# Attention queries: the second operand's marks and maxima transposed two heads at a time, its high parts copied by VectorE, and side b prepared further ahead

## The chip, the cores and the metric

One Trainium2 chip, one core. The metric is device time in microseconds of the whole kernel, one launch. Times of a kernel are the median of several executions; a profile is taken of one further execution, whose own time stands beside them.

## The reference

A decoder layer on 1024 tokens of 1024 channels. After an adaptive layer norm, one projection gives the queries, keys, values and gates of two attention branches. The NSA branch (8 heads, 2 key heads, here "side a") adds three attentions: over compressed keys, over the 8 blocks of 64 keys that the compressed scores pick, and over a window of 512. The SWA branch ("side b") has a window of 128 and one sink logit per head. Both are gated, merged, projected and normalised. What the change touches is the softmax of the last two kinds:

```python
s = einsum('bqghd,bkgd->bghqk', qb, kb) * dh ** -0.5
s = where(mask, s, NEG_INF)
p = softmax(concatenate([s, sink]))[..., :-1]   # side b; side a without sink
o = einsum('bghqk,bkgd->bqghd', p, vb)
```

All inputs and outputs are float32. The kernel computes in float32 accuracy by splitting operands in a high and a low part.

## The kernel before

The stages in time: projections of keys and compression (to 141 us), the attention of side a (to about 616 us), of side b (to about 726 us), then the branches' outputs, the merge and the last norm. Attention is the class `Att` (from L719). A unit is one side, one key head (group) and one tile of 128 queries, with 4 heads; there are 16 units in each side. Key tiles hold 128 keys.

Three things happen to each unit, each written as a generator that yields its estimated TensorE time:

- `C` (L744): the unit's queries `q` are split into a high part (ScalarE, L752) and a low part (GpSimd, L753) in `qat`; 4 transposes (L759) put both, heads side by side, into one PSUM bank; ScalarE copies it to `qa` (L761). ScalarE also copies `q` into columns 0 to 63 of `qbt` (L755). In side a, compressed attention and the selection follow, which write marks of the blocks that aren't selected to columns 64 to 79 of `qbt`.
- `M` (L829): scores with the queries as the stationary side (matmuls by L108, the helper of all matmuls), whose row maxima VectorE takes from the bank (L878) to `mx` and reduces into columns 80 and 81 of `qbt` (L882). 4 transposes of `qbt` (L890) fill one bank and ScalarE copies it to `qb` (L892). So `qb` holds q's high part, marks and maxima as rows.
- per key tile, `score` (L896): two matmuls, `qa` and `qb` against two operands of the keys, add up to the scores less the row maximum; on the diagonal and at the window's edge VectorE adds a mask (L907); ScalarE takes Exp (L909, L911) and the high part `ph` (L914), GpSimd the low part `pl` (L917). `weigh` (L920): 12 matmuls of `pl`, `ph` with V. `combine` (L940): VectorE divides by the sum.

`run` (L960) writes the order: at each step the score one step ahead, then parts of M of the next unit and of C of the unit behind it, then the weighing, and after each piece as much "fill" as a ratio asks: projections of queries, side b's keys (`kv_b`), and gate projections (`gm_block`, L1246, whose result `gmo` VectorE copies out and SP's queue writes). A framework then orders instructions by their dependences and puts semaphores. Banks 2 to 4 turn over among C, M and their transposes, 0 and 1 among the scores, 5 holds the weighed sums, 6 and 7 the fill. `qb` has 2 buffers, `qa` 3, `qbt` 2. The factor 0.125 of the scores is in the tables (`qcos`, `qsin`, L1173) with which queries are rotated. The core of `run`:

```python
            if ui + 1 < len(units):
                part(self.M, units[ui + 1], k, n)
            if ui + 2 < len(units):
                part(self.C, units[ui + 2], k, n)
```

Of the kernel before, what the change touches and what calls it, by code (L numbers as in the profile page):

```python
# [7 lines left out]
F32 = mybir.dt.float32  # L8
F32R = mybir.dt.float32r
# [4 lines left out]
OP = mybir.AluOpType  # L14
# [701 lines left out]
class Att:  # L716


    def __init__(self, L, q, work):  # L719

        self.L, self.q, self.w = L, q, work
        self.ms, self.st, self.av = Banks(L, MS), Banks(L, ST), Banks(L, (5,))
        nc = L.nc
        self.nc = nc
        self.U = {}
        self.qbt = []
        for i in range(2):
# [3 lines left out]
        self.p0 = work.tile([128, 128], F32, name="p0")[:, :68]  # L731
        nc.gpsimd.memset(self.p0, 0.0)
        self.n, self.last = 0, []
        self.off = [True, True]

    def rows_off(self, i):

        if not self.off[i]:
            self.nc.gpsimd.tensor_copy(self.qbt[i][:, :, 64:80],
                                       self.L.mk[:, 128:129, None].to_broadcast([128, 4, 16]))  # L740
            self.off[i] = True


    def C(self, u):  # L744
# [5 lines left out]
        self.n += 1  # L750
        qbt = st["qbt"] = self.qbt[self.n % 2]
# [8 lines left out]
        qa = st["qa"] = w.tile([128, 512], F32R, name="qa", tag="qa", bufs=3)  # L760
        nc.scalar.copy(qa, tr.bitcast(F32).rearrange("p h t -> p (h t)"))  # L761
        yield 0.25
        if side == "b":
            self.rows_off(self.n % 2)
# [5 lines left out]
        t = w.tile([128, 4, 64], F32, name="cs", tag="cs")  # L770
        nc.vector.tensor_tensor(t, sc[:, :, 1, :], L.vis[:, qt, None, :].to_broadcast([128, 4, 64]), op=OP.add)
        nc.vector.tensor_tensor(t, t, sc[:, :, 0, :], op=OP.add)
        sm = w.tile([128, 4, 8], F32, name="csm", tag="csm", bufs=2)[:, :, :4]
# [8 lines left out]
        pc = w.tile([128, 4, 64], F32, name="cp", tag="cp")  # L782
        nc.vector.scalar_tensor_tensor(pc.rearrange("p h c -> p (h c)"), e.rearrange("p h c -> p (h c)"), TINY,
# [5 lines left out]
        if qt >= 4:  # L789
            nc.vector.tensor_reduce(self.p0[:, 1:64], pc[:, :, 0:63].rearrange("p h c -> p c h"), axis=AX.X, op=OP.add)  # L790
            im = w.tile([128, 4, 16], F32, name="imp", tag="imp")
# [3 lines left out]
            m8 = w.tile([128, 40], F32, name="m8", tag="m8")[:, :8]  # L795
            nc.vector.max(m8, im[:, 1])
            nc.vector.match_replace(im[:, 2], m8, im[:, 1], -3e38)
            sel = st["sel"] = w.tile([128, 16], F32, name="sel", tag="sel", bufs=3)
            nc.vector.tensor_scalar(sel, im[:, 2], -2e38, NEG, op0=OP.is_gt, op1=OP.mult)
            nc.gpsimd.tensor_copy(qbt[:, :, 64:80], sel[:, None, :].to_broadcast([128, 4, 16]))  # L800
# [7 lines left out]
        pT = w.tile([128, 2, 128], F32, name="pT", tag="pT")  # L808
        nc.scalar.copy(pT, tp)
# [19 lines left out]
    def M(self, u):  # L829
        L, nc, w = self.L, self.nc, self.w  # L830
        side, g, qt = u
        st = self.U[u]
        qa, qbt = st["qa"], st["qbt"]
        brs = self.branches(u)
# [5 lines left out]
        for bi, (br, kts) in enumerate(brs):  # L840
# [10 lines left out]
            for a, b, hs in groups:  # L851
# [29 lines left out]
                yield 0.22 * (b - a) * len(hs) / 512  # L881
        nc.vector.tensor_reduce(qbt[:, :, 80:82], mx, axis=AX.X, op=OP.max, negate=True)  # L882
        if side == "b":
            es = st["es"] = w.tile([128, 2, 4], F32, name="esink", tag="esink", bufs=3)
            nc.gpsimd.tensor_tensor(es[:, 0], L.sink[:, g * 4:g * 4 + 4], qbt.bitcast(F32)[:, :, 80 + g], op=OP.add)
            nc.scalar.activation(es[:, 1], es[:, 0], AF.Exp, bias=L.poff)
        yield 0
        tr = self.ms.tile([128, 4, 128], F32R)
        for h in range(4):
            self.last.append(nc.tensor.transpose(tr[:, h, :], qbt[:, h, :], L.idr).ins)  # L890
        qb = st["qb"] = w.tile([128, 512], F32R, name="qb", tag="qb", bufs=2)
        nc.scalar.copy(qb, tr.bitcast(F32).rearrange("p h t -> p (h t)"))  # L892
        yield 0.25


    def score(self, u, br, kt):  # L896
# [9 lines left out]
        if kt == qt or edge:  # L906
            nc.vector.tensor_tensor(e.rearrange("p (h q) -> p h q", h=4), ps.rearrange("p (h q) -> p h q", h=4),  # L907
                                    L.mkt[:, int(edge), None, :].to_broadcast([128, 4, 128]), op=OP.add)
            nc.scalar.activation(e, e, AF.Exp, bias=L.poff)  # L909
        else:  # L910
            nc.scalar.activation(e, ps, AF.Exp, bias=L.poff)  # L911
        ph = w.tile([128, 512], F16, name="ph", tag="ph", bufs=PB)
# [47 lines left out]
    def run(self, units, fill, ratio, values):  # L960
# [80 lines left out]
        for gi, grp in enumerate(groups):  # L1041
# [24 lines left out]
            if k == n:  # L1066
                if ui + 1 < len(units):
                    finish(self.M, units[ui + 1])
                if ui + 2 < len(units):
                    finish(self.C, units[ui + 2])  # L1070
                self.U.pop(u)
                fill.done(u)
# [51 lines left out]
def run_layer(L):  # L1124
# [69 lines left out]
    def q_chunk(side, g, rows):  # L1194
# [322 lines left out]
```

## Time and profile before

| what | value |
|---|---|
| median of 3 runs | 943.93 us (943.79, 943.93, 946.45) |
| profiled execution | 945.29 us, of which the span of the core's instructions is 943.5 us |
| mean granted clock of TensorE in it | 0.994 of full speed |
| TensorE (PE) busy | 914.3 us |
| VectorE (DVE), ScalarE (ACT), GpSimd (POOL) busy | 550.2, 471.4, 575.6 us |

Busy times are of the one profiled execution; engines work side by side, so they don't add up to the span. PEld is TensorE's loading of stationary operands, which overlaps its matmuls. The granted clock (PEclk) is 1.00 at 2.4 GHz and 0.50 at 1.2 GHz.

### The profile page before, as it was taken

Reading aid. Unit: us, or ns where it says so; the run is one execution under the profiler, and the core shown is the slowest. Engines: PE = TensorE matmul, PEld = TensorE weight load, DVE = VectorE, ACT = ScalarE, POOL = GpSimd, SP = SyncE. Lnnn points to the kernel's source line nnn. Section 1 sums busy time; section 2 is a strip of 40 time slices with the busy share of each in tenths; the row PEclk is TensorE's granted clock in tenths of the full one; section 3 lists DMA queues with packets and bytes.
Section 4 is the critical chain, followed back from the end, with each engine's and each line's share of the span. In section 5 each row is a group of like instructions: output and inputs, shape, how many; then the busy total and the mean of one; then the engine's idle time right before and its main releaser. Section 6 shows DMA issues by size and latency. Waiting matters only on the chain.

```text
span 943.5 us, 18610 instructions
## 1 busy us (share of the span) xinstructions
PE 914.3 (97%) x6592; PEld 787.0 (83%) x6592; DVE 550.2 (58%) x1621; ACT 471.4 (50%) x984; POOL 575.6 (61%) x808
## 2 busy tenths in 40 slices
PE   7899998999999999999999999999899999999996
PEld 5689997788899888898899888789788888888885
DVE  7843356554776554465786643456552666454687
ACT  5846344344555566646555555756663664532100
POOL 7867565365768766767677766756753245535822
PEclk9999999999999999999999999999989999999999
DMA  9913232212202211202201212030222977655312
GB/s 329 293 29 115 81 91 57 79 51 79 68 7 53 62 57 57 63 13 70 76 7 35 74 58 75 22 101 13 69 62 75 371 249 221 192 188 193 130 69 110
DMA packets 93278, 95.40 MB, mean 101 GB/s; under 512 B 7616, under 2 KB 72192, under 8 KB 93184
## 3 DMA queue, kind: packets, MB, share of 16 engines
q1 hardware_dynamic: 93184, 94.21, 31.9%
q8 instruction: 52, 0.85, 0.4%
q14 instruction: 42, 0.34, 0.1%
HBM read 73.21 MB, written 20.97 MB: 100 GB/s over the span
## 4 chain that ended last, share of the span: by engine, by line
PE 69%; DMA 8%; DVE 8%; POOL 7%; ACT 3%; issue 3%; SPq 1%; DVEq 0%; POOLq 0%; ACTq 0%
PE bank L108 65%; DMA sg<-gm_raw 2%; POOL z L1421 2%; DMA raw<-in_w_ada_dram 2%; DMA raw<-in_w_out_dram 1%; DMA raw<-in_w_in_dram 1%; POOL rstd L1444 1%; DVE res L1450 1%; POOL pl L917 1%; PE bank L890 1%; DVE jk L878 1%; DMA x<-in_x_dram 1%; PE bank L759 1%; POOL whl L260 1%; PE bank L1327 1%
## 5 line engine op out<-in xcount | busy, mean ns | idle before, releaser
L108 PE MATMUL bank<-whl,uH 128*128 128x256 f32 (+3 forms) x1168 | 270.6, 322 | 4.6 <-ACT uH L449 4.3
L108 PE MATMUL bank<-uH,whl 128*128 128x512 f32 x768 | 247.5, 397 | 0.0
L917 POOL TENSOR_TENSOR pl<-e,ph 128x512 f16<-128x512 f32 x162 | 188.1, 1167 | 66.4 <-ACT ph L914 58.1
L108 PEld LDWEIGHTS bank<-whl,uH 128*128 128x128 f32 x1168 | 197.9, 189 | 22.2 <-ACT uH L449 5.3
L108 PE MATMUL bank<-whl,uL 128*128 128x256 f32 (+3 forms) x584 | 181.3, 319 | 0.0
L108 PEld LDWEIGHTS bank<-uH,whl 128*128 128x128 f32 x768 | 142.1, 189 | 26.8
L260 POOL TENSOR_TENSOR whl<-raw,whl 128x256 fp32r<-128x256 f32 x128 | 99.1, 779 | 86.6 <-ACT whl L259 78.6
L108 PE MATMUL bank<-uL,whl 128*128 128x512 f32 x384 | 151.3, 394 | 0.0
L108 PEld LDWEIGHTS bank<-whl,uL 128*128 128x128 f32 x584 | 110.1, 189 | 7.4
L914 ACT CAST ph<-e 128x512 f16<-128x512 f32 x162 | 98.4, 618 | 25.1 <-PE bank L108 23.1
L878 DVE CUSTOM_DVE_ANT_0 jk<-bank,mk 128x256 bf16<-128x256 f32 (+3 forms) x168 | 73.9, 440 | 30.0 <-PE bank L108 25.4
L911 ACT ACTIVATE e<-bank,poff 128x512 f32<-128x512 f32 x92 | 62.0, 687 | 54.0 <-PE bank L108 50.3
L108 PEld LDWEIGHTS bank<-uL,whl 128*128 128x128 f32 x384 | 72.6, 189 | 14.9
L259 ACT CAST whl<-raw 128x256 fp32r<-128x256 f32 x128 | 50.8, 404 | 66.0 <-PE bank L108 42.2
L108 PE MATMUL bank<-yH,whl 128*128 128x512 f32 x256 | 79.1, 393 | 0.0
L108 PEld LDWEIGHTS <-pl 128*128 128x128 f16 x648 | 59.4, 98 | 17.1 <-issue 11.2
L249 POOL TENSOR_TENSOR whl<-raw,whl 128x256 fp32r<-128x256 f32 (+3 forms) x60 | 53.3, 895 | 24.1 <-ACT whl L248 22.8
L907 DVE TENSOR_TENSOR e<-bank,mkt 128x512 f32<-128x512 f32 x70 | 47.5, 688 | 33.0 <-PE bank L108 27.9
L108 PEld LDWEIGHTS <-ph 128*128 128x128 f16 x1296 | 65.2, 97 | 0.8 <-issue 0.5
L909 ACT ACTIVATE e<-e,poff 128x512 f32<-128x512 f32 x70 | 49.8, 721 | 30.5 <-DVE e L907 30.2
L248 ACT CAST whl<-raw 128x256 fp32r<-128x256 f32 (+3 forms) x72 | 34.2, 480 | 60.9 <-DMA raw<-in_w_out_dram 36.8
L108 PEld LDWEIGHTS bank<-yH,whl 128*128 128x128 f32 x256 | 47.7, 188 | 10.1 <-issue 0.5
(292 smaller groups left out, 1730.0 us busy)
## 6 DMA issues: line engine op xcount, KB each, us to landing
raw<-in_w_in_dram SPq DMA_DIRECT2D x136, 128.0 KB, 2.2
gm_raw<-gmo SPq DMA_DIRECT2D x48, 256.0 KB, 2.0
wada<-in_w_ada_dram SPq DMA_DIRECT2D x16, 512.0 KB, 6.0
sg<-gm_raw SPq DMA_DIRECT2D x32, 256.0 KB, 3.2
x<-in_x_dram SPq DMA_DIRECT2D x8, 512.0 KB, 5.1
o_raw<-q SPq DMA_DIRECT2D x32, 128.0 KB, 1.9
o<-o_raw SPq DMA_DIRECT2D x8, 512.0 KB, 6.7
z<-gm_raw SPq DMA_DIRECT2D x16, 256.0 KB, 6.7
```

What stands on the lines that cost most here:

```text
L108: return self.nc.tensor.matmul(out, l, r, start=start, stop=stop, skip_group_check=True)
L248: self.cast = nc.scalar.copy(h, raw).ins
L249: low = eng.tensor_tensor(l, raw, h.bitcast(F32), op=OP.subtract).ins
L259: nc.scalar.copy(hl[:, 0], raw)
L260: eng.tensor_tensor(hl[:, 1], raw, hl.bitcast(F32)[:, 0], op=OP.subtract)
L878: nc.vector.tensor_tensor_reduce(o, src, m, 1.0, -3e38, OP.add, OP.max, mx[:, h, g if side == "b" else bi, slots[h]:slots[h] + 1])
L907: nc.vector.tensor_tensor(e.rearrange("p (h q) -> p h q", h=4), ps.rearrange("p (h q) -> p h q", h=4), L.mkt[:, int(edge), None, :].to_bro ...
L909: nc.scalar.activation(e, e, AF.Exp, bias=L.poff)
L911: nc.scalar.activation(e, ps, AF.Exp, bias=L.poff)
L914: nc.scalar.copy(ph, e)
L917: eng.tensor_tensor(pl, e, ph, op=OP.subtract)
L1421: nc.gpsimd.tensor_scalar(z[:, t, :], z[:, t, :], ALPHA, None, op0=OP.mult)
```

## The change

- `qbt` goes. Marks and maxima have a small tile `ex` of 32 columns per head (16 marks, 2 maxima, zeros), 2 of them in side a, 3 in side b. `qb` becomes a persistent buffer (3 in side a, 4 in side b) whose rows 64 to 127 are zeroed once by VectorE.
- The high parts, rows 0 to 63 of `qb`, are now copied by VectorE from C's transposed bank (64x512, L788 of the new kernel), the bank that ScalarE copies to `qa` (L787). ScalarE's cast of `q` (L755) goes.
- M's transposes take two heads at a time: 2 of 128x64 (L916) for 4 of 128x128; two VectorE copies of 32 rows and 2x128 columns (L920) put the result into `qb`, and ScalarE's copy (L892) goes. The yield of this piece is 0.14 for 0.25.
- The factor 0.125 moves from the rotation tables, which go with their three multiplications on ScalarE, into the `scale` of Exp; sinks are multiplied by 8 once on GpSimd.
- Some temporaries of side a lie in a pool of their own, closed at the first C of side b, where a second pool gives the additional `qb`, `ex` and `qa`.
- In side b a function `jobs` names what is written at which step: for unit ui the rest of M of ui+1, the score groups of M of ui+2, and C of ui+3. Before it was M of ui+1 and C of ui+2.

```diff
-        self.qbt = []
-        for i in range(2):
-            q = work.tile([128, 4, 128], F32R, name=f"qbt{i}")
-            nc.gpsimd.tensor_copy(q.rearrange("p h d -> p (h d)"), L.mk[:, 128:129].to_broadcast([128, 512]))
-            self.qbt.append(q)
+        self.ex = [work.tile([128, 4, 32], F32R, name=f"ex{i}") for i in range(2)]
+        self.qb = [work.tile([128, 512], F32R, name=f"qb{i}") for i in range(3)]
+        for x in self.ex:
+            nc.gpsimd.tensor_copy(x.rearrange("p h c -> p (h c)"), L.mk[:, 128:129].to_broadcast([128, 128]))
+        for x in self.qb:
+            nc.vector.tensor_copy(x[64:128], L.mk[64:128, 128:129].to_broadcast([64, 512]))
...
+        if side == "a":
+            ex, qb = self.ex[self.n % 2], self.qb[self.n % 3]
+        else:
+            if len(self.ex) == 2:
+                L.close(self.wx_cm)
+                self.wx, self.wx_cm = L.pool("sideb", 1, side="right")
+                self.qb.append(self.wx.tile([128, 512], F32R, name="qb3"))
+                self.ex.append(self.wx.tile([128, 4, 32], F32R, name="ex2"))
+                nc.gpsimd.tensor_copy(self.ex[2].rearrange("p h c -> p (h c)"), L.mk[:, 128:129].to_broadcast([128, 128]))
+                nc.vector.tensor_copy(self.qb[3][64:128], L.mk[64:128, 128:129].to_broadcast([64, 512]))
+                self.nb = 0
+            i = (1, 2, 0)[self.nb % 3]
+            if i < 2:
+                self.rows_off(i)
+            ex, qb = self.ex[i], self.qb[(2, 3, 0, 1)[self.nb % 4]]
+            st["n"] = self.nb
+            self.nb += 1
+        st["ex"], st["qb"] = ex, qb
         nc.scalar.copy(qat[:, :, 0, :], q)
...
-        (nc.gpsimd.tensor_copy if QL == 2 else nc.scalar.copy)(qbt[:, :, 0:64], q)
...
+        if side == "b" and st["n"] % 4 == 1:
+            qa = self.wx.tile([128, 512], F32R, name="qa3", tag="qa3")
+        else:
+            qa = w.tile([128, 512], F32R, name="qa", tag="qa", bufs=3)
+        st["qa"] = qa
         nc.scalar.copy(qa, tr.bitcast(F32).rearrange("p h t -> p (h t)"))
+        nc.vector.tensor_copy(qb[0:64], tr.bitcast(F32)[0:64].rearrange("p h t -> p (h t)"))
...
-        nc.scalar.activation(e, t, AF.Exp)
+        nc.scalar.activation(e, t, AF.Exp, scale=SCALE)
...
-        nc.vector.tensor_reduce(qbt[:, :, 80:82], mx, axis=AX.X, op=OP.max, negate=True)
+        nc.vector.tensor_reduce(ex[:, :, 16:18], mx, axis=AX.X, op=OP.max, negate=True)
...
-        tr = self.ms.tile([128, 4, 128], F32R)
-        for h in range(4):
-            self.last.append(nc.tensor.transpose(tr[:, h, :], qbt[:, h, :], L.idr).ins)
-        qb = st["qb"] = w.tile([128, 512], F32R, name="qb", tag="qb", bufs=2)
-        nc.scalar.copy(qb, tr.bitcast(F32).rearrange("p h t -> p (h t)"))
-        yield 0.25
+        tr = self.ms.tile([128, 2, 128], F32R)
+        for j in range(2):
+            self.last.append(nc.tensor.transpose(tr[0:64, j, :], ex[:, 2 * j:2 * j + 2, :].rearrange("p h c -> p (h c)"),
+                                                 L.idr).ins)
+        rows = qb[64:96].rearrange("p (j i t) -> p i j t", j=2, i=2)
+        for i in range(2):
+            nc.vector.tensor_copy(rows[:, i], tr.bitcast(F32)[i * 32:i * 32 + 32])
+        yield 0.14
...
+        def all_but(f, u):
+            s = get(f, u)
+            while s[1] < 3:
+                s[1] += 1
+                feed(next(s[0]))
...
+        def jobs(ui):
+            b = 2 * NT
+            if ui == b - 2:
+                return [(finish, self.C, b + 1, 0)]
+            if ui == b - 1:
+                return [(finish, self.M, b, -6), (finish, self.C, b + 2, -3), (all_but, self.M, b + 1, -1)]
+            if ui >= b:
+                e = EORD
+                return [(finish, self.M, ui + 1, e[0]), (all_but, self.M, ui + 2, e[1]), (finish, self.C, ui + 3, e[2])]
+            return []
 
...
-            if ui + 1 < len(units):
+            if ui < 2 * NT - 1:
                 part(self.M, units[ui + 1], k, n)
-            if ui + 2 < len(units):
                 part(self.C, units[ui + 2], k, n)
+            for f, g, x, w in jobs(ui):
+                if x < len(units) and k == (w if w > 0 else n + w):
+                    f(g, units[x])
...
+    nc.gpsimd.tensor_scalar(L.sink, L.sink, 1.0 / SCALE, None, op0=OP.mult)
...
-    L.qcos = qp.tile([128, 8, 32], F32, name="qcos")
-    qsin = qp.tile([128, 2, 8, 32], F32, name="qsin")
-    L.qsin = (qsin[:, 0], qsin[:, 1])
-    for o, x in ((L.qcos, L.cos), (L.qsin[0], L.nsin), (L.qsin[1], L.sin)):
-        nc.scalar.mul(o, x, 0.125)
```

TensorE's instructions in side b, in the kernel before (`K·qa` as `qa,Kw` with 512 columns is the first score matmul, `qb,Kw` the second; `Kw,qa` are M's scores; `whl`, `uH`, `uL` are fill):

```order
L108 MATMUL bank_10418<-Kw_934,qa 128x256 x2
L108 MATMUL bank_10386<-uL,whl 128x512
L759 MATMUL bank_10472<-idr,qat 128x128 x4
L108 MATMUL bank_10459<-qa,Kw_934 128x512
L108 MATMUL bank_10502<-qa,Kw_934 128x512
L108 MATMUL bank_10518<-Kw_934,qa 128x256 x2
L890 MATMUL bank_10452<-idr,qbt_1882 128x128 x4
L759 MATMUL bank_10583<-idr,qat 128x128 x4
L108 MATMUL bank_10459<-qb,Kw_934 128x512
L108 MATMUL bank_10502<-qb,Kw_934 128x512
L108 MATMUL bank_10525<-Kw_934,qa 128x256 x2
```

Here C's transposes into bank_10472 stand three rows ahead of M's scores into bank_10518, which read the copy of that bank. And after the change, again in side b (L781 are C's transposes, L916 M's, of `ex`):

```order
L110 MATMUL bank_10482<-qb_1881,Kw_930 128x512
L110 MATMUL bank_10421<-uH,whl 128x512 x2
L110 MATMUL bank_10421<-uL,whl 128x512
L110 MATMUL bank_10421<-uH,whl 128x512 x2
L110 MATMUL bank_10421<-uL,whl 128x512
L110 MATMUL bank_10421<-uH,whl 128x512 x2
L110 MATMUL bank_10421<-uL,whl 128x512
L110 MATMUL bank_10527<-qa,Kw_930 128x512
L781 MATMUL bank_10503<-idr,qat 128x128 x4
L110 MATMUL bank_10588<-qa,Kw_930 128x512
L110 MATMUL bank_10543<-Kw_930,qa_10369 128x256 x2
L916 MATMUL bank_10492<-idr,ex_1879 64x128 x2
```

M's scores into bank_10543 read a `qa` whose transposes stand 69 rows earlier, with two steps' weighing and 18 fill matmuls between; the C at L781 between them belongs to a later unit. VectorE's instructions at a place in side b, before (`jk,mx` are M's maxima):

```order
L878 ISA jk,mx<-bank_10411,mk 128x256
L878 ISA mx 128x1
L878 ISA jk,mx<-bank_10411,mk 128x256
L878 ISA mx 128x1
L907 TENSOR_TENSOR e<-bank_10318,mkt 128x512
L907 TENSOR_TENSOR e<-bank_10395,mkt 128x512
L878 ISA jk,mx<-bank_10418,mk 128x256
L878 ISA mx 128x1
L878 ISA jk,mx<-bank_10418,mk 128x256
L878 ISA mx 128x1
```

Maxima and the masked adds of scores (`e`) take turns. After the change:

```order
L904 ISA jk,mx<-bank_10441,mk 128x256
L904 ISA mx 128x1
L920 CAST qb_1881<-bank_10356 32x2x128 x2
L788 CAST qb_8285<-bank_10364 64x512
L904 ISA jk,mx<-bank_10441,mk 128x256
L904 ISA mx 128x1
L935 TENSOR_TENSOR e<-bank_10425,mkt 128x512
L904 ISA jk,mx<-bank_10448,mk 128x256
L904 ISA mx 128x1
L976 TENSOR_TENSOR cf<-bank_10378,esink 128x4
L935 TENSOR_TENSOR e<-bank_10482,mkt 128x512
```

The new copies into `qb` stand between the maxima of one bank, and ahead of the masked add that follows.

## Rows read from the trace of the kernel before

**Rows 1.** Page, part 1: busy us (share of the span) xinstructions.

```profile
span 943.5 us, 18610 instructions
...
PE 914.3 (97%) x6592; PEld 787.0 (83%) x6592; DVE 550.2 (58%) x1621; ACT 471.4 (50%) x984; POOL 575.6 (61%) x808
```

**Rows 2.** Page, part 4: the chain that ended last, by engine.

```profile
PE 69%; DMA 8%; DVE 8%; POOL 7%; ACT 3%; issue 3%; SPq 1%; DVEq 0%; POOLq 0%; ACTq 0%
```

**Rows 3.** Stretches: length, busy us PE PEld DVE ACT POOL, PEclk, DMA, GB/s.

```profile
199.00:616.00 417.00, 415.66 (x3625) 359.62 (x3624) 242.68 (x872) 238.70 (x474) 289.49 (x378) 1.00 0.18 53
616.00:726.00 110.00, 105.50 (x909) 92.22 (x908) 57.21 (x211) 61.95 (x131) 63.88 (x102) 0.97 0.19 54
```

**Rows 4.** The same view, finer, in side b.

```profile
679.00:683.30 4.30, 2.08 (x13) 1.28 (x11) 2.46 (x10) 2.93 (x7) 2.42 (x6) 1.00 0.51 122
683.30:690.15 6.85, 6.46 (x29) 5.43 (x30) 3.17 (x10) 5.17 (x12) 5.73 (x9) 0.50 0.01 2
690.15:726.00 35.85, 35.44 (x285) 29.44 (x285) 15.07 (x54) 16.99 (x35) 15.52 (x21) 1.00 0.20 60
```

**Rows 5.** TensorE's waits, 616 to 726 us: total us, times, longest us.

```profile
PE bank L108 <- ACT qa L761: 1.5, 1, 1.5
PE bank L890 <- DVE qbt L882: 1.4, 3, 0.7
PE bank L759 <- DVE mx L878: 1.0, 1, 1.0
```

**Rows 6.** Timeline of TensorE: start us, us, instruction [idle before <-releaser].

```profile
679.02 0.46 PE L759 MATMUL bank<-idr,qat 128*128 128x128 f32 x4
679.32 1.06 PE L108 MATMUL bank<-qa,Kw 128*128 128x512 f32 x2
681.92 0.50 PE L108 MATMUL bank<-Kw,qa 128*128 128x256 f32 x2 [1.55 <-ACT qa L761]
682.26 0.45 PE L890 MATMUL bank<-idr,qbt 128*128 128x128 f32 x4
683.69 0.72 PE L759 MATMUL bank<-idr,qat 128*128 128x128 f32 x4 [0.97 <-DVE mx L878]
```

**Rows 7.** Timeline of TensorE in side b, at M's transposes.

```profile
645.32 0.46 PE L890 MATMUL bank<-idr,qbt 128*128 128x128 f32 x4
645.62 0.20 PE L108 MATMUL bank<-Vs,pl 128*128 128x65 f16 x1
```

**Rows 8.** Instructions on qbt: ns min/median/max, first and last start.

```profile
L890 PEld LDWEIGHTS bank<-idr,qbt x128: 138/141/147, 184.5 to 713.9; 128*128 128x128 f32 x128
```

**Rows 9.** Groups by line and form, whole span: busy us, mean ns | idle before.

```profile
L892 ACT CAST qb<-bank 128x512 fp32r<-128x512 f32 x32 | 18.8, 586 | 22.4 <-PE bank L890 22.2
...
L761 ACT CAST qa<-bank 128x512 fp32r<-128x512 f32 x32 | 18.6, 581 | 7.0 <-PE bank L759 6.8
...
L755 ACT CAST qbt<-q 128x256 fp32r<-128x256 f32 x32 | 13.1, 409 | 0.1
...
L310 DVE CAST Kw<-bank 64x256 fp32r<-64x256 f32 x12 | 5.1, 427 | 5.8 <-ACT Kw L309 5.6
...
L907 DVE TENSOR_TENSOR e<-bank,mkt 128x512 f32<-128x512 f32 x70 | 47.5, 688 | 33.0 <-PE bank L108 27.9 <-POOL pl L917 2.7 <-POOL mx L839 1.8
...
L909 ACT ACTIVATE e<-e,poff 128x512 f32<-128x512 f32 x70 | 49.8, 721 | 30.5 <-DVE e L907 30.2
...
L914 ACT CAST ph<-e 128x512 f16<-128x512 f32 x162 | 98.4, 618 | 25.1 <-PE bank L108 23.1
...
L917 POOL TENSOR_TENSOR pl<-e,ph 128x512 f16<-128x512 f32 x162 | 188.1, 1167 | 66.4 <-ACT ph L914 58.1 <-DVE mx L878 1.7 <-POOL pl L917 1.4
```

**Rows 10.** TensorE's waits, 141.5 to 199 us.

```profile
PE bank L108 <- ACT qa L761: 0.7, 1, 0.7
PE bank L890 <- DVE qbt L882: 0.6, 1, 0.6
```

**Rows 11.** Who waited for ScalarE's casts of L309, from keys' banks: us, times.

```profile
  DVE Kw L310: 5.6, 6
```

**Rows 12.** Groups of VectorE, 616 to 726 us.

```profile
L907 DVE TENSOR_TENSOR e<-bank,mkt 128x512 f32<-128x512 f32 x26 | 17.3, 687 | 9.1 <-PE bank L108 7.0 <-POOL mx L839 1.8 <-POOL pl L917 0.2
```

More of the change, by code (lines that the diff above doesn't have):

```diff
@@ L28 @@
 POFF = math.log(16.0)
+SCALE = 0.125
+EORD = (1,0,1)
 XB = 8
@@ L725, in __init__ @@
         self.U = {}
-        self.qbt = []
-        for i in range(2):
-            q = work.tile([128, 4, 128], F32R, name=f"qbt{i}")
-            nc.gpsimd.tensor_copy(q.rearrange("p h d -> p (h d)"), L.mk[:, 128:129].to_broadcast([128, 512]))
-            self.qbt.append(q)
+        self.ex = [work.tile([128, 4, 32], F32R, name=f"ex{i}") for i in range(2)]
[4 more added lines that the diff above has]
+            nc.vector.tensor_copy(x[64:128], L.mk[64:128, 128:129].to_broadcast([64, 512]))
         self.p0 = work.tile([128, 128], F32, name="p0")[:, :68]
+        self.wx, self.wx_cm = L.pool("sidea", 1, side="right")
         nc.gpsimd.memset(self.p0, 0.0)
@@ L738, in rows_off @@
         if not self.off[i]:
-            self.nc.gpsimd.tensor_copy(self.qbt[i][:, :, 64:80],
+            self.nc.gpsimd.tensor_copy(self.ex[i][:, :, 0:16],
                                        self.L.mk[:, 128:129, None].to_broadcast([128, 4, 16]))
@@ L750, in C @@
         self.n += 1
-        qbt = st["qbt"] = self.qbt[self.n % 2]
+        if side == "a":
[16 more added lines that the diff above has]
+        st["ex"], st["qb"] = ex, qb
         nc.scalar.copy(qat[:, :, 0, :], q)
@@ L769, in C @@
                              L.kcd[:, g].rearrange("p i c -> p (i c)"), True, True).ins)
-        t = w.tile([128, 4, 64], F32, name="cs", tag="cs")
+        t = self.wx.tile([128, 4, 64], F32, name="cs", tag="cs")
         nc.vector.tensor_tensor(t, sc[:, :, 1, :], L.vis[:, qt, None, :].to_broadcast([128, 4, 64]), op=OP.add)
         nc.vector.tensor_tensor(t, t, sc[:, :, 0, :], op=OP.add)
-        sm = w.tile([128, 4, 8], F32, name="csm", tag="csm", bufs=2)[:, :, :4]
+        sm = self.wx.tile([128, 4, 8], F32, name="csm", tag="csm", bufs=2)[:, :, :4]
         nc.vector.tensor_reduce(sm[:, 0], t, axis=AX.X, op=OP.max)
@@ L781, in C @@
         nc.gpsimd.tensor_tensor(e, e, sm[:, 2, :, None].to_broadcast([128, 4, 64]), op=OP.mult)
-        pc = w.tile([128, 4, 64], F32, name="cp", tag="cp")
+        pc = self.wx.tile([128, 4, 64], F32, name="cp", tag="cp")
         nc.vector.scalar_tensor_tensor(pc.rearrange("p h c -> p (h c)"), e.rearrange("p h c -> p (h c)"), TINY,
@@ L790, in C @@
             nc.vector.tensor_reduce(self.p0[:, 1:64], pc[:, :, 0:63].rearrange("p h c -> p c h"), axis=AX.X, op=OP.add)
-            im = w.tile([128, 4, 16], F32, name="imp", tag="imp")
+            im = self.wx.tile([128, 4, 16], F32, name="imp", tag="imp")
             nc.vector.tensor_reduce(im[:, 0], self.p0[:, 0:64].rearrange("p (j i) -> p j i", i=4), axis=AX.X, op=OP.add)
@@ L794, in C @@
             nc.gpsimd.tensor_tensor(im[:, 1], im[:, 0], L.forced[:, qt], op=OP.add)
-            m8 = w.tile([128, 40], F32, name="m8", tag="m8")[:, :8]
+            m8 = self.wx.tile([128, 80], F32, name="m8", tag="m8")[:, :8]
             nc.vector.max(m8, im[:, 1])
             nc.vector.match_replace(im[:, 2], m8, im[:, 1], -3e38)
-            sel = st["sel"] = w.tile([128, 16], F32, name="sel", tag="sel", bufs=3)
+            sel = st["sel"] = self.wx.tile([128, 16], F32, name="sel", tag="sel", bufs=3)
             nc.vector.tensor_scalar(sel, im[:, 2], -2e38, NEG, op0=OP.is_gt, op1=OP.mult)
-            nc.gpsimd.tensor_copy(qbt[:, :, 64:80], sel[:, None, :].to_broadcast([128, 4, 16]))
+            nc.gpsimd.tensor_copy(ex[:, :, 0:16], sel[:, None, :].to_broadcast([128, 4, 16]))
             self.off[self.n % 2] = False
@@ L807, in C @@
             self.last.append(nc.tensor.transpose(tp[:, j, :], pc[:, 2 * j:2 * j + 2, :].rearrange("p h c -> p (h c)"), L.idf).ins)
-        pT = w.tile([128, 2, 128], F32, name="pT", tag="pT")
+        pT = self.wx.tile([128, 2, 128], F32, name="pT", tag="pT")
         nc.scalar.copy(pT, tp)
@@ L832, in M @@
         st = self.U[u]
-        qa, qbt = st["qa"], st["qbt"]
+        qa, ex, qb = st["qa"], st["ex"], st["qb"]
         brs = self.branches(u)
@@ L881, in M @@
                 yield 0.22 * (b - a) * len(hs) / 512
-        nc.vector.tensor_reduce(qbt[:, :, 80:82], mx, axis=AX.X, op=OP.max, negate=True)
+        nc.vector.tensor_reduce(ex[:, :, 16:18], mx, axis=AX.X, op=OP.max, negate=True)
         if side == "b":
-            es = st["es"] = w.tile([128, 2, 4], F32, name="esink", tag="esink", bufs=3)
-            nc.gpsimd.tensor_tensor(es[:, 0], L.sink[:, g * 4:g * 4 + 4], qbt.bitcast(F32)[:, :, 80 + g], op=OP.add)
-            nc.scalar.activation(es[:, 1], es[:, 0], AF.Exp, bias=L.poff)
+            es = st["es"] = w.tile([128, 2, 8], F32, name="esink", tag="esink", bufs=3)[:, :, :4]
+            nc.gpsimd.tensor_tensor(es[:, 0], L.sink[:, g * 4:g * 4 + 4], ex.bitcast(F32)[:, :, 16 + g], op=OP.add)
+            nc.scalar.activation(es[:, 1], es[:, 0], AF.Exp, bias=L.poff, scale=SCALE)
         yield 0
-        tr = self.ms.tile([128, 4, 128], F32R)
-        for h in range(4):
-            self.last.append(nc.tensor.transpose(tr[:, h, :], qbt[:, h, :], L.idr).ins)
-        qb = st["qb"] = w.tile([128, 512], F32R, name="qb", tag="qb", bufs=2)
-        nc.scalar.copy(qb, tr.bitcast(F32).rearrange("p h t -> p (h t)"))
-        yield 0.25
+        tr = self.ms.tile([128, 2, 128], F32R)
[6 more added lines that the diff above has]
+        yield 0.14
     def score(self, u, br, kt):
@@ L908, in score @@
                                     L.mkt[:, int(edge), None, :].to_broadcast([128, 4, 128]), op=OP.add)
-            nc.scalar.activation(e, e, AF.Exp, bias=L.poff)
+            nc.scalar.activation(e, e, AF.Exp, bias=L.poff, scale=SCALE)
         else:
-            nc.scalar.activation(e, ps, AF.Exp, bias=L.poff)
+            nc.scalar.activation(e, ps, AF.Exp, bias=L.poff, scale=SCALE)
         ph = w.tile([128, 512], F16, name="ph", tag="ph", bufs=PB)
@@ L1066, in run @@
             if k == n:
-                if ui + 1 < len(units):
+                if ui < 2 * NT - 1:
                     finish(self.M, units[ui + 1])
-                if ui + 2 < len(units):
                     finish(self.C, units[ui + 2])
@@ L1203, in q_chunk @@
             q = qp.tile([128, 256], F32, name="q", tag="q", bufs=QB)
-            L.rope(q, a[:, :256], t, qp, nc.vector, L.qcos, L.qsin)
+            L.rope(q, a[:, :256], t, qp, nc.vector)
             rows[side, g, t] = q
@@ L1300, in run_layer @@
     fill.rest()
-    for cm in (wk_cm, kvb[0], k0_cm, k1_cm, qp_cm):
+    for cm in (A.wx_cm, wk_cm, kvb[0], k0_cm, k1_cm, qp_cm):
         L.close(cm)
```

2 lines of the change are left out of this document (removed).

## The prediction, on record before the result

> **What bounds the kernel now.** I read four views in this order: busy time, chain of waits, stretches by stage, and waits inside the stage that the change reorders. TensorE is busy for 97% of the span while no other engine passes 61% [rows 1], and 69% of the chain that ended last is TensorE, with VectorE at 8%, GpSimd at 7% and ScalarE at 3% [rows 2]. So work counts if TensorE does it or has to wait for it. The stretches say where TensorE has room [rows 3]: in side a (199 to 616 us) it is busy 415.66 of 417.00 us, in side b (616 to 726 us) 105.50 of 110.00, so side b holds 4.5 us of idle time and side a 1.3. The finer stretches [rows 4] show what that idle time brings with it: from 679.00 to 683.30 TensorE is busy for 2.08 of 4.30 us, and in the 6.85 us behind it the granted clock is 0.50, that is 1.2 GHz for 2.4, with TensorE busy 6.46 us. Then it is 1.00 again. The waits of side b [rows 5] name the causes: 1.5 us on ScalarE's copy of `qa` (L761), 1.4 on VectorE's reduction into `qbt` (L882), 1.0 on the maxima that held a bank (L878). They lie at one place [rows 6]: C's transposes at 679.02, the marks of the next unit that need the copy of those very transposes at 681.92 (1.55 us waited), then at 683.69 the next C, waiting for a bank that M's maxima still read (0.97 us). The written order had put C, M and the next C back to back, with nothing between them to cover the round trips.
>
> **Fewer transposes.** M now issues two transposes of 128x64 for four of 128x128. The multiset of TensorE's instructions is otherwise the same, so 2 x 32 units = 64 transposes go. The four start 0.30 us before the next matmul [rows 7], 0.075 each; two new ones should take 0.15, since they move the same 128 columns of output each. 64 x 0.075 = 4.8 us, half of it in side a, where TensorE has no idle time to swallow it. From above I bound it by the weight load, 0.141 us each [rows 8], or 9.0; from below by nothing, if the shorter transposes pace as two old ones. I take 4.8, the measured pace.
> The Trainium skill ("TensorE: Matmul & The Clock Gate", section "Part 4: PE-mode transpose") gives about 275 ns for a transpose in one kernel's context; an estimate by that page is 64 x 0.275 = 17.6 us. The trace's 0.075 differs from it, and the measurement decides.
>
> **Side b's order.** In before each M stands as little as three rows behind the C that makes its `qa`; after the change C runs three units ahead and M two, with weighing and fill matmuls between (the order excerpts). If the longer distances cover the round trip, the 2.2 us of idle time in 679.00 to 683.30 shrink, and with it the half clock: 6.46 us of work at 1.2 GHz would take 3.2 at 2.4, so **3.2 us** come back [rows 4]. The bounds are 0 (the idle time moves elsewhere and the clock falls there) and 3.2. Of the 4.5 us of idle time itself I take **2.0**, which is less than the 3.9 us of waits in rows 5, because some new stall will take the place of the old ones; the bounds are 0 and 4.5. I stay below half because scores still need VectorE, ScalarE and GpSimd in turn before a step can be weighed.
>
> **ScalarE relieved.** 32 casts into `qbt` (L755) and 32 copies to `qb` (L892) go, 13.1 + 18.8 = 31.9 us [rows 9]. ScalarE is at 50% and on 3% of the chain, so TensorE hides it: 0. Should the waits on `qa` and `qbt` in the first units (141.5 to 199 us) shorten with it, 0.7 + 0.6 = 1.3 us come back [rows 10]; this is a lower end only. The three multiplications for scaled rotation tables, the smaller initialisation on GpSimd and the scale moved into Exp and the sinks count nothing: they lie on engines at 50% and 61% [rows 1], and TensorE's work is the cover; if that cover failed, each is a fraction of a microsecond, once.
>
> **VectorE burdened.** Each unit gains a copy of 64x512 from C's bank into `qb` and two of 32x256 from M's. A 128x512 masked add from a bank takes 0.688 us and a 64x256 cast from one 0.427 [rows 9], both with the same columns as the new copies. So 32 x 0.69 + 64 x 0.42 = 49 us more on VectorE, 58% to 63% of the span. Four fills of zeros (4 x 0.69 = 2.8 us) come once. **Added wait:** the 64x512 copy reads the bank that ScalarE is copying to `qa`, and is made to wait for it; behind it on VectorE stand maxima of M and masked adds. Before, two engines did read one bank in turns: VectorE waited 5.6 us for ScalarE's `Kw` over 6 casts [rows 11]. Who needs the copy is the second score matmul alone, which in side b now stands two units later, and in side a a whole unit's steps later. Cover: the fill matmuls and other steps' weighing. I take 0; if the wait is paid in full in side b it is one `qa` copy per unit, 16 x 0.58 = 9.3 us [rows 9].
>
> **The sum.** 4.8 + 3.2 + 2.0 = 10.0 us. The profiled execution took 945.29 us (span 943.5 and 1.8 around it), so 935.3 on its scale. It is 1.4 above the median of the three runs (943.93), so against the median **933.9 us**.
>
> **Rivals.**
> (1) *Only the transposes count.* The waits find another place in side b, and the half clock with them: the reordering only shifts who is late, as 105.50 of 110.00 is already close. For: the queue of transfers and fill is the same. Against: the two waits of rows 6 have one cause, steps written back to back, that the order removes. 943.93 - 4.8 = 939.1.
> (2) *ScalarE's copy is paid twice.* VectorE's copy, held behind ScalarE's on the same bank, holds back the maxima and with them the bank; 9.3 us come on top of the forecast: 933.9 + 9.3 = 943.2, no change. For: the turns of rows 11. Against: side b has more distance now, and side a's TensorE waits only 1.3 us in all.
> The Trainium skill ("PSUM — Partial Sum Buffer", section "Terms") states that two engines may not be on the same bank and partitions at once, reads against reads included; rows 11 agree, and by that rule the copy can't run beside ScalarE's.
> (3) *Slower: VectorE's queue in side b.* There it is busy 57.21 of 110 us [rows 3]; with 16 units' 1.53 us it comes to 82. The copies stand between maxima and ahead of masked adds (order excerpt), and 26 masked adds fall in that stretch [rows 12]. If each of the 26 waits behind two copies, half of it exposed, 26 x 0.42 = 10.9 us are added, and the half clock remains: 943.93 - 4.8 + 10.9 = 950.0. It decides once VectorE's backlog is longer than what lies between a score and its weighing: add, Exp, high and low part take 0.69 + 0.72 + 0.62 + 1.17 = 3.2 us [rows 9], and scores run one step ahead only. Against: two copies make 0.85 us, a quarter of that, and 28 us of side b stay free on VectorE.
> (4) *The change doesn't save TensorE's time:* the two new transposes pace at 0.15 us each, so the pair takes as long as the four did, and only the order counts (3.2 + 2.0): 943.93 - 5.2 = 938.7.
>
> **How the numbers follow.** About 0.3%, 2.8 us, is what a measurement of this kernel can tell from no change, so faster means under 941.1 and slower over 946.8. Chances: the forecast 0.55, rival 1 0.22, rival 2 0.12, rival 3 0.08, rival 4 0.03. Faster is 0.55 + 0.22 + 0.03 = 0.80, same 0.12, slower 0.08. The range starts at 929.5, 4.4 below the forecast, which takes in most of what the bounds leave below it (4.2 of transposes, 2.5 of idle time, 1.3 at the start, not all at once), and ends at 941.5, which holds rivals 1 and 4 and leaves out 2 and 3, 0.20 together.
>
> **What would show it.** Right: 64 transposes of M at about 0.15 us a pair; no stretch of clock 0.50 in side b; its idle time under 3 us and its length near 102; VectorE near 600 us busy; side a shorter by about 2.4. Wrong: a new stretch at half clock (rival 1); TensorE waiting for `qb` behind VectorE, whose copy waits for ScalarE (rival 2); masked adds that start late, with matmuls waiting for `pl` or `ph` (rival 3); M's transposes pacing at 0.15 each (rival 4).

## The result, and the profile after

The changed kernel takes 934.51 us (median of 4 runs, 934.21 to 934.94) against 944.77 for the kernel before (4 runs): 10.26 us less, a ratio of 0.9891 with a 95% interval of 0.9876 to 0.9905 (8.9 to 11.7 us). The forecast was 933.9, 10.0 us less than the 943.93 that three of the four runs before had given.

The page's busy times and its chain by engine, of the changed kernel:

```profile
span 932.5 us, 18523 instructions
...
PE 906.2 (97%) x6528; PEld 777.6 (83%) x6528; DVE 598.6 (64%) x1721; ACT 446.1 (48%) x917; POOL 574.3 (62%) x810
...
PE 86%; DVE 7%; POOL 2%; ACT 2%; DMA 1%; issue 1%; SPq 0%; DVEq 0%; POOLq 0%; ACTq 0%
```

Against [rows 1] TensorE has 64 matmuls and 8.1 us less, VectorE 48.4 us more (49 were forecast), ScalarE 25.3 less. The chain is TensorE for 86%, not 69% [rows 2].

The stretches by stage are cut at the same instructions in both kernels: the first weighing matmul, side b's first, the last, and the first matmul of the outputs behind. First the kernel before:

```profile
190.32:615.15 424.83, 423.49 (x3671) 366.04 (x3671) 246.38 (x882) 242.80 (x482) 294.17 (x384) 1.00 0.18 52
615.15:724.37 109.22, 104.72 (x915) 91.64 (x915) 57.24 (x211) 62.68 (x133) 64.73 (x103) 0.97 0.20 58
724.37:757.03 32.66, 32.66 (x175) 27.56 (x172) 18.39 (x31) 18.44 (x34) 7.11 (x9) 1.00 0.93 325
```

The changed kernel:

```profile
189.33:613.23 423.90, 422.16 (x3641) 362.85 (x3641) 274.29 (x946) 229.34 (x447) 293.73 (x387) 1.00 0.18 51
613.23:716.50 103.27, 102.47 (x900) 89.51 (x900) 70.68 (x239) 53.35 (x108) 65.04 (x102) 1.00 0.23 65
716.50:746.05 29.55, 29.55 (x159) 25.00 (x156) 16.12 (x28) 15.45 (x29) 5.33 (x7) 1.00 0.93 338
```

Side b is 5.95 us shorter and TensorE's idle time in it went from 4.50 to 0.80 us; its clock is 1.00 throughout. The stage behind is 3.1 us shorter, since 12 fill matmuls of it (and 12 from earlier stages) now lie in side b. So stage lengths alone mislead here. I therefore split each stage in two: the *pace* of its matmuls (for each form the median distance from one start to the next, over both traces, times how many there are; M's and C's transposes and the keys' also by their place in a run of them) and the *excess* over it (idle time, half clock, slower issue).

| stage | pace before, after | excess before, after |
|---|---|---|
| first C to first weighing | 40.6, 39.6 | 6.6, 6.7 |
| side a | 409.9, 406.2 | 14.9, 17.7 |
| side b | 96.6, 98.5 | 12.7, 4.8 |
| from there to the last matmul on `yL` | 121.7, 118.9 | 0.7, 0.7 |

Pace fell by 5.6 us in all, the transposes' part. Excess fell by 7.9 us in side b, and rose by 2.8 in side a. These are differences of one execution of each kernel. The expectations below were written with all old transposes at their common median, 0.085 us, which makes it 6.9, 7.3 and 3.5. That median misleads, since the distances fall in two groups and it lies in the dearer one. Median distances in us from one start to the next, by place in a run:

| transposes | first | second | third | fourth |
|---|---|---|---|---|
| M's old ones, 128x128, runs of four (before) | 0.061 | 0.066 | 0.085 | 0.089 |
| C's, 128x128, runs of four (after) | 0.060 | 0.063 | 0.086 | 0.087 |
| keys' (`khl`), 128x128, runs of two (before) | 0.060 | 0.063 | | |
| M's new ones, 128x64, runs of two (after) | 0.060 | 0.062 | | |

A run of the old four takes 0.302 us in the median, as [rows 7] showed it, and the new pair 0.124.

TensorE's waits in side b, 613 to 716.5 us, against [rows 5]:

```profile
PE bank L110 <- DVE mx L904: 0.5, 1, 0.5
PE bank L110 <- DVE qb L920: 0.2, 1, 0.2
```

At the entry to side a one wait of TensorE has grown. Stretches there, of the changed kernel and then of the kernel before:

```profile
186.00:188.50 2.50, 1.11 (x5) 0.68 (x5) 2.43 (x12) 2.50 (x5) 1.11 (x2) 1.00 0.01 3
188.50:192.00 3.50, 3.08 (x19) 2.48 (x20) 2.84 (x9) 0.47 (x2) 3.27 (x5) 0.52 0.00 0
```

```profile
186.00:188.50 2.50, 1.87 (x6) 0.94 (x6) 2.03 (x6) 2.27 (x6) 0.74 (x1) 1.00 0.21 50
188.50:192.00 3.50, 2.69 (x26) 2.37 (x27) 2.88 (x13) 1.92 (x4) 2.92 (x5) 1.00 0.00 0
```

TensorE's timeline there, in the changed kernel and then before:

```profile
187.33 0.63 PE L110 MATMUL bank<-kcd,qa 128*128 128x128 f32 x4 [0.86 <-DVE mx L904]
188.60 0.41 PE L916 MATMUL bank<-idr,ex 128*64 128x128 f32 x2 [0.63 <-DVE ex L908]
189.33 0.24 PE L110 MATMUL bank<-Vs,pl 128*128 128x65 f16 x1 [0.32 <-POOL pl L945]
```

```profile
188.68 0.63 PE L108 MATMUL bank<-kcd,qa 128*128 128x128 f32 x4 [0.40 <-DVE mx L878]
189.94 0.54 PE L890 MATMUL bank<-idr,qbt 128*128 128x128 f32 x4 [0.63 <-DVE qbt L882]
```

VectorE is busy 2.43 of 2.50 us while TensorE waits for its maxima, 0.86 us for 0.40 before, and in the 3.5 us behind it TensorE's clock is at 1.2 GHz. The kernel before has the same two waits and 1.00 behind them in this trace. But that half clock is not a mark of the change. The old operands in the new order have it too (190 us), and the held run of one transpose, which has the new operands, has not; both runs are described below. First the former, then the latter:

```profile
187.00:190.00 3.00, 1.89 (x18) 1.33 (x18) 2.86 (x13) 2.02 (x5) 1.72 (x3) 1.00 0.01 3
190.00:193.50 3.50, 3.50 (x18) 2.82 (x15) 1.68 (x7) 1.25 (x3) 2.73 (x5) 0.51 0.00 0
```

```profile
186.00:188.50 2.50, 1.26 (x6) 0.81 (x6) 2.43 (x12) 2.50 (x5) 1.14 (x2) 1.00 0.01 3
188.50:192.00 3.50, 2.80 (x23) 2.31 (x23) 2.90 (x10) 0.47 (x2) 3.29 (x5) 1.00 0.00 0
```

M's new transposes, between two halves of another unit's C:

```profile
652.59 0.28 PE L916 MATMUL bank<-idr,ex 128*64 128x128 f32 x2
652.71 0.32 PE L781 MATMUL bank<-idr,qat 128*128 128x128 f32 x2
```

Two take 0.12 us, where four took 0.30 [rows 7]. And VectorE does wait for ScalarE on the shared bank (VectorE's waits, 199 to 726 us):

```profile
DVE qb L788 <- ACT qa L787: 11.4, 9, 2.4
```

### The profile page after: what moved, and what is told of

Same layout as the page of the kernel before. It is cut to its first block, busy times and chain, and to the rows that moved or that the text cites. A ratio compares the mean times of both kernels' runs of the same rounds, so it can differ in the third digit from the quotient of the medians.

```text
span 932.5 us, 18523 instructions
## 1 busy us (share of the span) xinstructions
PE 906.2 (97%) x6528; PEld 777.6 (83%) x6528; DVE 598.6 (64%) x1721; ACT 446.1 (48%) x917; POOL 574.3 (62%) x810
## 4 chain that ended last, share of the span: by engine, by line
PE 86%; DVE 7%; POOL 2%; ACT 2%; DMA 1%; issue 1%; SPq 0%; DVEq 0%; POOLq 0%; ACTq 0%
PE bank L110 82%; POOL rstd L1489 1%; DVE res L1495 1%; PE bank L781 1%; DMA x<-in_x_dram 1%; PE bank L1372 1%; DVE jk L904 1%; DVE stats L1481 1%; DVE z L1480 1%; DVE gt L1479 1%; DVE lnst L534 1%; ACT lnT L448 0%; DMA raw<-in_w_in_dram 0%; DVE qb L920 0%; DVE e L935 0%
## 5 line engine op out<-in xcount | busy, mean ns | idle before, releaser
L110 PEld LDWEIGHTS bank<-whl,uH 128*128 128x128 f32 x1168 | 197.1, 189 | 21.8 <-ACT uH L451 5.2
```

The lines of the kernel that those rows point to most:

```text
L110: return self.nc.tensor.matmul(out, l, r, start=start, stop=stop, skip_group_check=True)
```

## The experiments

Each was compared with the kernel before on the same chip; its median there was 945.1 to 945.5 us, and the ratios to it have intervals of at most 0.0019 to either side. The changed kernel wasn't run again beside them: "over the changed kernel" is against its 934.51, where the kernel before took 944.77. So such a difference is known to some 2 us only. Each run was traced once.

**The new operands with the old order.** In `run`, side b's jobs are undone:

```diff
-            if ui < 2 * NT - 1:
-                part(self.M, units[ui + 1], k, n)
-                part(self.C, units[ui + 2], k, n)
-            for f, g, x, w in jobs(ui):
...
+            if ui + 1 < len(units):
+                part(self.M, units[ui + 1], k, n)
+            if ui + 2 < len(units):
+                part(self.C, units[ui + 2], k, n)
```

> The new operands (two transposes per unit, VectorE's copies, ex and qb) with side b written in the order of before: M one unit ahead, C two. Theory (transposes and order are separate gains): only the order's gain is lost, which the two profiles put at 7.3 us of excess time in side b (12.0 before, 4.7 after), so 934.5 + 7.3 = 941.8, and a stretch of clock 0.50 in side b is back. Rival (the operands' own shorter round trip, one VectorE copy instead of ScalarE's after four transposes, removed the stalls, and the order did little): within 2 us of 934.5.

940.42 us, 5.9 over the changed kernel. Its stretches in side b:

```profile
664.00:670.00 6.00, 3.74 (x22) 2.70 (x21) 5.29 (x18) 3.35 (x7) 3.53 (x7) 1.00 0.07 25
670.00:674.00 4.00, 4.00 (x30) 3.85 (x30) 2.15 (x7) 2.88 (x5) 2.39 (x5) 0.57 0.00 0
```

and TensorE's waits there:

```profile
667.62 0.47 PE L110 MATMUL bank<-Kw,qa 128*128 128x256 f32 x2 [0.86 <-DVE mx L904]
669.49 0.74 PE L110 MATMUL bank<-qb,Kw 128*128 128x512 f32 x2 [1.28 <-DVE qb L920]
```

A stall, then half clock, as in [rows 4, 6], now with VectorE's copy in ScalarE's place. The operands don't remove the stalls; the order does. Side b's excess is 11.1 us here.

**The old operands with the new order.** The jobs are put into the kernel before, with a third `qbt` and a fourth `qa` in side b:

```diff
-        qbt = st["qbt"] = self.qbt[self.n % 2]
+            i = (1, 2, 0)[self.nb % 3]
...
+        qbt = st["qbt"] = self.qbt[i]
```

> The operands of before (qbt, four transposes of 128x128, ScalarE's cast and copy, three qbt in side b) with side b written in the order of the change: M two units ahead, C three. Theory: the order alone gives its 7.3 us and none of the transposes' 6.9, and side a doesn't give back the 3.5 us of excess that the changed kernel has there: 944.8 - 7.3 = 937.5, side b without half clock. Rival (operands did it): within 2 us of 944.8.

940.76 us, 4.4 less than before. Side b's idle time fell to 2.46 us (103.02 long, TensorE 100.56 busy), and its clock was 1.00. Its excess is 7.4 us, between the 12.7 before and the 4.8 of the change. So the direction held and the size did not: some waits remain, the longest for VectorE's maxima. One line is of ScalarE's copy to `qb`, which the new operands replace, and one of its copy to `qa`, which they keep (waits of 616.6 to 719.7 us):

```profile
PE bank L109 <- DVE mx L897: 0.9, 1, 0.9
PE bank L109 <- ACT qb L911: 0.5, 2, 0.3
PE bank L909 <- ACT qa L781: 0.5, 1, 0.5
```

The two halves, 4.8 and 4.4, add up to 9.2 of 10.3, which is the whole within the interval.

**The high parts on ScalarE.**

```diff
-        nc.vector.tensor_copy(qb[0:64], tr.bitcast(F32)[0:64].rearrange("p h t -> p (h t)"))
+        nc.scalar.copy(qb[0:64], tr.bitcast(F32)[0:64].rearrange("p h t -> p (h t)"))
```

> The changed kernel, but the high parts of qb (64x512 from C's bank) are copied by ScalarE, right behind its copy to qa, and not by VectorE. Theory (VectorE's added work delays maxima and masked adds in side a's first units and costs the 3.5 us of excess there): 931.0 to 932.8, no half clock at 188 us. Rival A (VectorE's work is covered, the excess of side a is chance): 934.5 within 1. Rival B (ScalarE, with Exp and the high parts of scores, becomes late): 936 or more.

938.91 us: slower, as rival B. Half clock lasted 6.8 us at 188 us, so taking this copy from VectorE did not cure that stall. What made it slower isn't shown: this edit moved the order too (see the next run).

**Four transposes of 128x32.**

```diff
-        for j in range(2):
-            self.last.append(nc.tensor.transpose(tr[0:64, j, :], ex[:, 2 * j:2 * j + 2, :]...
+        for h in range(4):
+            self.last.append(nc.tensor.transpose(tr[0:32, h, :], ex[:, h, :], L.idr).ins)
```

> The changed kernel, but M transposes one head at a time: four transposes of 128x32 for two of 128x64, VectorE's two copies of the same 32x256 size kept. So 64 transposes are added and nothing else. Theory: TensorE pays the pace of each, 0.062 us as the two pace now: +4.0, 938.5. The forecast's price of 0.075 would give +4.8, 939.3; the price that the profiles' difference shows (6.9 us for 64) +6.9, 941.4. Rival (the transposes are not on the path): 934.5 within 1.

941.30 us, 6.8 over the changed kernel. But the edit did more than it says: the framework orders instructions by its own estimates. Of TensorE's 6528 instructions in the changed kernel's trace only 5723 stand in one common sequence with this run's (by form, without buffer numbers); with the kernel before it is 5587. I come back to this below.

**The copy twice, from SBUF, on GpSimd, and one transpose for four heads.** Four edits of the same lines: VectorE's copy of 64x512 written twice; its source `qa` instead of the bank; the same on GpSimd; and M's transposes as one:

```diff
+        nc.vector.tensor_copy(qb[0:64], qa.bitcast(F32)[0:64])
...
+        nc.gpsimd.tensor_copy(qb[0:64], qa.bitcast(F32)[0:64])
...
+        self.last.append(nc.tensor.transpose(tr, ex.rearrange("p h c -> p (h c)"), L.idr).ins)
+        for h in range(4):
+            nc.vector.tensor_copy(rows[:, h], tr.bitcast(F32)[h * 32:h * 32 + 32])
```

> The changed kernel with VectorE's copy of 64x512 from C's bank written twice, to the same place: 32 x 0.68 = 21.8 us more on VectorE, and the bank is held 0.68 us longer in each unit. Theory (VectorE's added 49 us are nearly covered, what they cost is in the first units alone): 934.5 to 936.0. Rival (VectorE's backlog delays masked adds and maxima wherever it is busy): a second helping of nearly half the added work costs at least half of what a per-unit delay costs, 32 x 0.68 / 2 = 10.9, so 940 or more.

942.89 us, as the rival had it.

> The changed kernel, but VectorE copies the high parts from ScalarE's result qa in SBUF and not from the bank: the wait for ScalarE stays, but the bank is free 0.68 us sooner in each unit, and the copy itself reads no bank. Theory (the turns on the shared bank are covered): 934.5 within 1. Rival (the bank held by a second reader delays what goes into the ring of three banks): 931.5 to 933.5, and fewer waits of TensorE for banks in 141 to 199 us.

935.21 us: within 1, as the theory said. The bank held longer costs nothing that these runs can tell.

> The changed kernel, but GpSimd copies the high parts from qa in SBUF: VectorE has 21.8 us less, GpSimd some 20 more (a fill of 128x512 took it 0.6 us in the kernel before). Theory A (VectorE's added work costs about 2 us of the excess in side a): 932.5 to 933.5. Theory B (it is covered; GpSimd, on which the low parts of scores wait, is the tighter one): 935 to 938.

942.41 us, 7.9 over the changed kernel and beyond what either theory gave.

> The changed kernel, but M transposes all four heads of ex at once, one transpose of 128x128 for two of 128x64; VectorE then copies four times 32x128 (0.29 us each by the maxima of that width, 1.16 us for 0.84 per unit). Theory (transposes are paid on TensorE at 0.06 us of pace, and up to 0.107 with what four instead of two cost): 934.5 - 32 x 0.06 to 0.107 = 931.1 to 932.6, faster than both kernels. Rival (the pace of one larger transpose is that of two, or VectorE's 10 us more eat it): 934.5 or more.

940.31 us: 32 transposes fewer, and 5.8 us slower than the changed kernel. Three of these four changed by 6 to 8 us, and in each of them (5863, 5694 and 5845 of 6528 TensorE instructions in a common sequence) much had moved. In the copy from `qa` as much had moved (5948), and it cost nothing. So these runs did not separate the cost of the edit from that of another order.

**The same with the order held.** So the last four chain every engine's instructions, by dependences that order issue alone, in the changed kernel's own order; added ones stand right behind their neighbours:

```diff
+    for k in order:
+        for i in [plain[k]] + [by[n] for n in EXTRA.get(plain[k].name, ())]:
+            if e in last:
+                tc.add_manual_dep(i, last[e], ..., reason="held order")
+            last[e] = i.name
```

In their traces the sequence of every engine is the changed kernel's, but for the edited instructions. A run that holds the order and edits nothing is missing.

> Four transposes per unit again for two, as in the earlier run, but now every engine's instructions are held in the changed kernel's order by explicit dependences, the two added ones right behind their neighbours. The earlier run cost 6.8 us, of which the paces of the 64 transposes make 3.8 and the rest may be the order, which the scheduler had written anew. Theory (the order was the rest): 934.5 + 3.8 = 938.3, at most 939.3. Rival (four of them cost more than their own pace, 0.107 each): 941.3.

938.22 us, 3.7 over the changed kernel: the theory. That it fits to 0.1 is luck, as the difference is known to 2 us. A run of four takes 0.240 us here, so the pace gives 32 x (0.240 - 0.124) = 3.7. The other 3.1 us of the earlier 6.8 were order.

> VectorE's copy of 64x512 written twice, as in the earlier run (8.4 us), in the changed kernel's order: only VectorE's queue grows, by 32 x 0.68 = 21.8 us. Theory (the 8.4 were mostly another order): 934.5 to 937. Rival (VectorE's backlog itself delays TensorE): 940 or more, with TensorE waiting for maxima, masked adds or the copies of VectorE in side a.

939.01 us: 4.5 for 21.8 us of VectorE's work, between the two. Of the earlier 8.4, then, some 4 were order and some 4 VectorE's queue. Part of the latter is the clock: in this trace the half clock at 188.9 us lasts 6.8 us, where the changed kernel's lasted 3.4, which makes 1.7. TensorE's longest wait in side b is behind VectorE's maxima (waits of 613 to 726 us), 1.4 us for the changed kernel's 0.5:

```profile
PE bank L111 <- DVE mx L907: 1.4, 1, 1.4
```

Its other new waits are behind ScalarE's Exp and high parts in side a, 1.1 and 1.6 us; what delays those the rows don't say.

> The changed kernel in its own order with VectorE's copy of the high parts left out (rows 0 to 63 of qb stay zero, so the scores lack the product of queries' high parts with the second key operand): VectorE has 21.8 us less and never waits for ScalarE on the shared bank. It prices that copy. Theory (covered, but for the first units' stall): 932.5 to 934.5. Rival (each of VectorE's microseconds is partly exposed, as the doubled copy's 8.4 for 21.8 would have it): 926 to 930.

935.88 us (934.33 to 937.23): leaving out 21.8 us of VectorE's work gained nothing, or at most 1 us within the interval. The copy is covered. TensorE's wait for maxima at the entry to side a is 0.40 us again, as before the change, and the half clock was there all the same:

```profile
188.50:192.00 3.50, 3.04 (x18) 2.56 (x19) 2.34 (x8) 0.42 (x1) 2.98 (x6) 0.50 0.00 0
```

> A candidate to beat both kernels, in the changed kernel's order: one transpose of 128x128 for all four heads (32 fewer, at a pace of 0.06 us: 1.9 us less on TensorE), four copies of 32x128 at 0.286 us for two of 0.42 (0.30 us more on VectorE per unit), and the high parts copied from qa in SBUF (0.456 us for 0.682, 0.23 less per unit). Theory (the earlier trial of one transpose, 940.3, lost its gain to another order): 934.5 - 1.9 = 932.6. Rival (four dependent copies at the end of M's chain are late): 935 or more, TensorE waiting for qb.

935.84 us (933.67 to 937.60): no better than the changed kernel. Its trace is of the fastest execution, 933.67, so it doesn't explain the median. In it the pace is 1.9 us shorter as expected, and the excess 1.7 longer, though there is no half clock in side a: TensorE waits for `qb` and the maxima (two lines of its waits, 613 to 726 us):

```profile
PE bank L111 <- DVE mx L905: 0.8, 1, 0.8
PE bank L111 <- DVE qb L921: 0.6, 1, 0.6
```

No run's median beat the changed kernel.

## Why the prediction was right

The sum, 10.0 us, came out at 10.3, but its terms were off in both directions. That it fits so closely is in part luck: in the two traces two terms were too small, and one that was put at nothing took from them.

- *Fewer transposes, 4.8 us.* Under-sized by about 0.9. The step that failed is the price of what stays. The old four take 0.302 us, as the prediction read from one place; but the new pair takes 0.124 and not 0.15, so 32 x (0.302 - 0.124) = 5.7. The prediction gave every transpose the mean of a run of four, and the two that go are its dear ones, 0.085 and 0.089. The shape alone doesn't make a pair cheap: the keys' 128x128 ones are as fast in runs of two, and the held run's single 128x128 ones take 0.0625, with weight loads of 141 ns against 110 for 128x64. But four of 128x32 take 0.060 each in the other held run, so the dear places belong to longer runs of 128x128. Why, no run shows. That count and pace set the price, once the order is held, is borne out by the held run of four (3.7 us for 3.7, to some 2 us). The 17.6 us worked out by the Trainium skill's 275 ns per transpose ("TensorE: Matmul & The Clock Gate", section "Part 4: PE-mode transpose") is far from both.
- *Side b's order, 3.2 + 2.0 us.* Right in cause, shown by the order undone (stall and half clock back, 5.9 us) and by the order alone (4.4 us, half clock in side b gone). By these runs the size is about right too. By the two traces it is larger: idle time fell by 3.7 us, not 2.0, because hardly any new stall took its place, and with the half clock the excess fell by 7.9. The half clock, though, differs between executions of one kernel. Those of the kernel before with a mean clock of 0.997 took 943.3 to 943.9 us, those with the profile's 0.994 took 945.0 to 945.8, so about 1.8 us apart. No trace shows which stretch the former lacked.
- *VectorE's added work, 0.* Right for the copy of 64x512: leaving it out gains nothing. The turn on the shared bank exists, 11.4 us of VectorE's waiting, but nobody needs the copy in that time (rival 2 falls). Rival 3's mechanism, VectorE's backlog, is real one step further on: 21.8 us more cost some 4.
- *Side a, 0 beyond its transposes.* Wrong: its excess rose by 2.8 us. 1.4 of this is the half clock from 189.3 to 192, half of those 2.7 us, which is not the change's, as shown above. With half clock taken off, side a's excess is 14.9 us before and 14.5 with the old operands in the new order; it is 16.3 in the changed kernel, 16.7 with the new operands in the old order, and 16.2 in the held runs of four transposes and without the copy. So about 1.5 us comes with the operands; it isn't the high parts' copy. Whether it is the two copies behind M's transposes, the smaller changes that came with them, or the order that the framework wrote around them was not tried, and stays open.
- Rivals 1 and 4 fall with the runs of the order and of the transposes.

## What to carry to other kernels

Where one engine is busy for 97% of the time, price its instructions by their start-to-start distance over the whole trace, by operand shape and by place in a run (a median over a mixture misled here), and add the idle time and the half clock that a stall drags along: both halves of this gain were found that way. Take a stall's cure from distance in program order between a producer and the engine that needs its round trip. And where a scheduler writes the order, an edit is two experiments in one until the order is held: of 6.8 and 8.4 us seen here, some 3 and 4 were only order.

## What the runs showed of the hardware

- VectorE's copy from SBUF to SBUF (64x512, fp32) is fast and unsteady. With `qa` as its source it took 0.41 us at best, 0.456 in the median, but 1.50 at most in the run of that edit alone, and in the held run of one transpose once 5.28, where from the bank it took 0.65 to 0.69 each time. GpSimd's timeline in that run, in the stretch of VectorE's copy at 517.47 us:

```profile
517.47 5.28 DVE L789 CAST qb<-qa 64x512 fp32r<-64x512 f32 x1 [1.08 <-ACT qa L788]
522.67 0.41 DVE L905 CUSTOM_DVE_ANT_1 jk<-bank,sel 128x256 bf16<-128x256 f32 x1
```

```profile
516.98 1.15 POOL L949 TENSOR_TENSOR pl<-e,ph 128x512 f16<-128x512 f32 x1
518.10 0.73 POOL L777 TENSOR_TENSOR qat<-q,qat 128x256 fp32r<-128x256 f32 x1
...
521.32 1.15 POOL L949 TENSOR_TENSOR pl<-e,ph 128x512 f16<-128x512 f32 x1
522.98 0.73 POOL L263 TENSOR_TENSOR whl<-raw,whl 128x256 fp32r<-128x256 f32 x1 [0.52 <-ACT whl L262]
```

  GpSimd ran without a pause until 522.47 us, and the copy ended at 522.75, 0.28 behind. The shorter ones of over 0.44 us have the same form: nearly all end some 0.28 us behind the GpSimd instruction that ran when they started, or the one right behind it. The Trainium skill ("GPSIMD Engine Reference", section "1. Specifications") says that GpSimd shares its SBUF interfaces with VectorE, with contention for some of VectorE's modes. These rows agree with the sharing; in which mode the copy ran they don't say. A copy that reads a bank is slower here and doesn't wait.
- In a run of TensorE's fp32 transposes of 128x128 the first two take some 0.06 us from start to start and the third and fourth some 0.086; four of 128x32 take 0.060 each.
- TensorE's clock fell to 1.2 GHz for 3.4 or 6.8 us at a time, in several places; in the three shown here (side b before, side b with the old order, side a after) TensorE had been idle for a third or more of the stretch ahead. That is not enough for a rule: in the held run of one transpose it was idle for half of the 2.5 us from 186.0 (busy 1.26), and the clock stayed at 1.00. Executions of the kernel before had mean clocks from 0.988 (948.19 us) to 0.997 (943.31 us) without any edit.
